# Gates and branches with the tokens stationary and 512 weight columns moving, the merged result turned on TensorE, and column sums and mixer steps placed anew

## The chip, the cores and the metric

One core of one Trainium2 chip runs the whole kernel. The metric is device time of one execution in microseconds (us), as the median of several executions. A profiled execution is slightly different from the timed ones; its own time stands beside its span below. Engines are called as the profile calls them: PE is TensorE (PEld its weight loads), DVE is VectorE, ACT is ScalarE, POOL is GpSimd, SP is SyncE, which issues the large loads.

## The reference, cut to what matters

256 tokens of width 2048 pass one encoder layer. All arithmetic is float32.

```
mod = silu(c) @ w_ada + b_ada                 # sh1, sc1, g1, sh2, sc2, g2, each 2048 wide
u = plain_norm(x) * (1 + sc1) + sh1
parts = split(u @ w_in)                       # inputs of the four mixers
y_a, y_b, y_c, y_d = pool(..), dsa(..), mla(..), conv(..)      # 512 wide each
gated = [sigmoid(u @ w_gate[i] + b_gate[i]) * (y @ w_branch[i])  for i, y in enumerate(...)]
merged = gated[0] + gated[1] + gated[2] + gated[3]
x = layer_norm(ALPHA * x + (1 + g1) * (merged @ w_o))
u2 = plain_norm(x) * (1 + sc2) + sh2
x = layer_norm(ALPHA * x + (1 + g2) * (silu(u2 @ wa) * (u2 @ wb)) @ w_ffn_out)
```

## The kernel before, in words

**Weights as a stream.** Weights come in loads of 1 MB (128 x 2048 float32) into three `raw` buffers (`RAW`). SP issues them in one fixed order (L1212). Each 128 x 1024 half of a load is one *unit*: ACT casts it to `wh` (L1242), DVE subtracts to get the rest `wl` (L1243), and PE multiplies high by high, high by low and low by high, so that each product of float32 matrices is three of fp32r. The preparation runs four units ahead of PE (`LEAD`), in five `wh` and five `wl` buffers. Every engine takes its instructions in the order in which this program writes them.

**Two ways to multiply.** `mm_B` (L393) keeps weights stationary and moves 256 tokens: 24 matmuls of 256 columns a unit, with features on the partitions of the result. `mm_A` (L418) keeps 128 tokens stationary and moves 512 weight columns: 12 matmuls of 512 columns a unit, with tokens on the partitions. `w_o` and the FFN go by `mm_A`; nearly all of `w_in`, the gates and the branches go by `mm_B`.

**The stages.** (1) The start: `w_ada` for sh1 and sc1 arrives in five segments among the first `w_in` units. DVE and POOL scale and sum its rows into `accd` and `accp`; PE turns the sum into columns (`adacol`, L263), DVE adds the bias (`modc`, L270 and L272), and `make_u` writes the high and low halves of u (`u0h`, `u0l`, ...), which all further units of those k need. (2) The rest of `w_in`, some 50 units, with the mixers beside it. The gate of branch 0 is computed here too (groups g of 10 and more). (3) Branch 0, then gate and branch of i = 3, 2 and 1: 48 loads of gates and 16 of branches, 128 units. (4) `w_o` and a norm. (5) The FFN.

**The ada rest.** 48 more loads of `w_ada` (the list `rest`) are strewn among the loads by `put_rest`, from load number `REST_FROM` of `w_in` on. For each load ACT scales two rows (L245, `gemv`) and POOL adds them to `accp` (L246).

**Side work.** The mixers are generators. After each unit, `run_side` advances each lane's first mixer; `yield n` means that its next step comes n units later (times the lane's pace), and `fins` holds the column sums, which run `FIN_DELAY` units after the sum is complete. A step puts its instructions on the engines' queues at that point of the program: a PE instruction of a step that is not ready holds all matmuls behind it. Column sums of squares (`rq`, `rkv`, `cvar`) are followed by a power on POOL (L151), a diagonal on DVE (L176) and a broadcast matmul on PE (`rbq`, `rbkv`, `cb`, L585).

**Slots.** Tiles of 128 x 1024 come from 30 slots; `drop` gives one back.

Of the kernel before, what the change touches and what calls it, by code (L numbers as in the profile page):

```python
# [74 lines left out]
def block_kernel(ctx: ExitStack, tc: tile.TileContext, a, out, dbg=None):  # L75
# [68 lines left out]
    bgh = cp.tile([P, 64], F32, name="bgh")  # L144
    dve.tensor_scalar(bgh, col("b_gate", 0, 64), 0.5, None, op0=OP.mult)
# [75 lines left out]
    def ada_items(srcs, width, on_dve, fin):  # L221
# [3 lines left out]
        def prep(i):  # L225
            def f(raw):
# [20 lines left out]
                if i == len(srcs) - 1:  # L247
# [6 lines left out]
                    fins.append([now[0] + FIN_DELAY, fin(ac), 1])  # L254
# [188 lines left out]
    def win_use(pi, g, k0, k1):  # L443
        def use(k, wh, wl):
# [6 lines left out]
            if g == 3:  # L451
# [37 lines left out]
    def gate_tanh(i, g, dst, src):  # L489
        for j in range(4):  # L490
            o = slice(j * 256, (j + 1) * 256)
            c = 16 * i + 4 * g + j
            act.activation(dst[:, o], src[:, o], AF.Tanh, scale=0.5, bias=bgh[:, c:c + 1])
# [4 lines left out]
    def seg_ada(si):  # L498
# [4 lines left out]
        return ada_items([a["ada1"][n0 + j] for j in range(n)], 512 if si < 2 else 1024, dv, seg_fin(si))  # L503
# [84 lines left out]
    def conv_mix():  # L588
# [34 lines left out]
        yield 2  # L623
# [44 lines left out]
    def rms(cq, nt, width, gname, name):  # L668
# [7 lines left out]
        yield 2  # L676
# [115 lines left out]
    def dsa_mix():  # L792
        iw, kp = idx["iw"], idx["kp"]
        yield 2
        sc_ = slot("score")
# [59 lines left out]
        drop(sc_, G.pop(1), G.pop(2), G.pop(3))  # L855
# [18 lines left out]
    def gate_use(i, g, kq):  # L874
        def use(half, wh, wl):
# [5 lines left out]
            mm_B(ps, wh, wl, act_u, ks, kq == 0 and half == 0, last)  # L881
            if last:
                T[i, g] = slot("T")
                gate_tanh(i, g, T[i, g], ps)
        return use

    def branch_use(i, g, first_i, last_i):
        def use(half, wh, wl):
# [500 lines left out]
```

## Time and profile before

| | us |
|---|---|
| median of 3 executions | 1735.74 |
| lowest and highest | 1734.02, 1741.04 |
| the profiled execution | 1733.01 |
| its span | 1731.2 |
| mean granted TensorE clock, share of full | 0.969 |

The span runs from the first to the last instruction. The page says how long each engine was busy, the windows say it for a stretch of time together with the granted clock and the DMA share, and the waits name who ended an engine's idle time. A matmul's duration overlaps the next, so the price of one is taken from start to start.

### The profile page before, as it was taken

To read this page: it belongs to the slowest core of one execution; us is meant where nothing else is said; L and a number is where in the kernel's file an instruction comes from. 1 tells how busy PE (TensorE), PEld (TensorE's weight loads), DVE (VectorE), ACT (ScalarE), POOL (GpSimd) and SP (SyncE) were. 2 spreads that over 40 slices of the span, in tenths; PEclk is the share of its full clock that TensorE was granted. 3 is DMA by queue.
4 is the path that set the end of the run, shared out by engine and by line. 5 is a ranking of instruction groups with operands and counts; after the bars stand their busy time and mean duration, and the time that the engine had idled before them with its cause. 6 is when DMAs were issued, how large, how long until landed. Compare 5 with 4: busy or idle time off the path is not lost.

```text
span 1731.2 us, 23941 instructions
## 1 busy us (share of the span) xinstructions
PE 1627.8 (94%) x9822; PEld 1462.7 (84%) x9822; DVE 1184.7 (68%) x1087; ACT 855.3 (49%) x1008; POOL 434.1 (25%) x194
## 2 busy tenths in 40 slices
PE   5789998977999999999999699999999999999996
PEld 5789998967999999989988588888888888888885
DVE  7698859895698698786766756676455555444556
ACT  5744545655666646656544454444443344444442
POOL 2422305664345575585302200000000000000001
PEclk8899989998999999999999799999999999999998
DMA  8877854464567667678666257777555555555661
GB/s 323 309 286 269 310 208 158 154 233 146 214 231 301 254 251 265 272 283 327 255 259 253 96 189 276 286 270 284 178 194 195 194 195 183 184 191 195 226 231 53
DMA packets 57854, 397.40 MB, mean 230 GB/s; under 512 B 6416, under 2 KB 6672, under 8 KB 11792
## 3 DMA queue, kind: packets, MB, share of 16 engines
q1 hardware_dynamic: 57456, 395.63, 62.3%
q8 instruction: 77, 1.26, 0.3%
q10 hardware_dynamic: 288, 0.23, 0.0%
q14 instruction: 33, 0.27, 0.0%
HBM read 393.74 MB, written 2.10 MB: 229 GB/s over the span
## 4 chain that ended last, share of the span: by engine, by line
PE 74%; DVE 10%; DMA 5%; issue 5%; ACT 3%; POOL 3%; ACTq 0%; DVEq 0%; POOLq 0%; SPq 0%
PE ffn L415 9%; PE ffn L416 9%; PE ffn L413 9%; PE tok L415 6%; PE tok L416 6%; PE tok L413 6%; PE gate L406 5%; PE gate L399 5%; PE gate L400 5%; DVE wl L1243 4%; DMA raw<-in_win_dram 4%; PE win L400 2%; PE win L399 2%; PE branch L399 2%; PE branch L406 2%
## 5 line engine op out<-in xcount | busy, mean ns | idle before, releaser
L1243 DVE TENSOR_TENSOR wl<-raw,wh 128x1024 fp32r<-128x1024 f32 x529 | 741.8, 1422 | 400.3 <-ACT wh L1242 399.4
L1242 ACT CAST wh<-raw 128x1024 fp32r<-128x1024 f32 x536 | 548.5, 1044 | 585.9 <-PE ffn L416 229.9
L246 POOL TENSOR_TENSOR accp<-accp,gemv 128x1024 f32<-128x1024 f32 (+1 forms) x118 | 322.8, 2736 | 321.7 <-ACT gemv L245 317.7
L151 POOL TENSOR_TENSOR rs_r<-rs_v,nhalf 128x1 f32<-128x1 f32 (+1 forms) x11 | 7.4, 676 | 785.5 <-DVE rs_v L149 785.5
L245 ACT ACTIVATE gemv<-raw,c_act 128x1024 f32<-128x1024 f32 (+1 forms) x118 | 128.3, 1122 | 55.8 <-DMA raw<-in_ada_dram 49.2
L240 DVE SCALAR_TENSOR_TENSOR accd<-raw,c_act,accd 128x1024 f32<-128x1024 f32 (+1 forms) x73 | 106.4, 1458 | 3.4 <-DMA raw<-in_ada_dram 2.1
L415 PE MATMUL ffn<-wl,v01h 128*128 128x512 f32 x176 | 69.8, 397 | 5.0 <-DVE wl L1243 5.0
L413 PE MATMUL ffn<-wh,v00h 128*128 128x512 f32 x176 | 71.4, 405 | 0.6 <-ACT v00h L1072 0.6
L416 PE MATMUL ffn<-wh,v00l 128*128 128x512 f32 x176 | 69.6, 396 | 1.5 <-DVE v00l L1074 1.5
L413 PE MATMUL ffn<-wh,v01h 128*128 128x512 f32 x176 | 70.2, 399 | 0.0
L413 PE MATMUL ffn<-wh,v10h 128*128 128x512 f32 x176 | 68.6, 390 | 1.4 <-ACT v10h L1072 1.4
L415 PE MATMUL ffn<-wl,v00h 128*128 128x512 f32 x176 | 69.5, 395 | 0.0
L416 PE MATMUL ffn<-wh,v01l 128*128 128x512 f32 x176 | 69.5, 395 | 0.0
L416 PE MATMUL ffn<-wh,v10l 128*128 128x512 f32 x176 | 68.6, 390 | 0.0
L415 PE MATMUL ffn<-wl,v10h 128*128 128x512 f32 x176 | 68.5, 389 | 0.0
L413 PE MATMUL ffn<-wh,v11h 128*128 128x512 f32 x176 | 68.5, 389 | 0.0
L415 PE MATMUL ffn<-wl,v11h 128*128 128x512 f32 x176 | 68.5, 389 | 0.0
L416 PE MATMUL ffn<-wh,v11l 128*128 128x512 f32 x176 | 68.5, 389 | 0.0
L399 PE MATMUL win<-u0h,wh 128*128 128x256 f32 x200 | 53.5, 301 | 13.8 <-ACT u0h L380 11.2
L610 POOL TENSOR_TENSOR cv<-cv,gemv 128x512 f32<-128x512 f32 x30 | 47.8, 1593 | 72.4 <-ACT gemv L608 71.6
L606 DVE SCALAR_TENSOR_TENSOR cv<-pad,wdw,cv 128x256 f32<-128x256 f32 x60 | 57.4, 996 | 0.0
L399 PE MATMUL win<-u1h,wh 128*128 128x256 f32 x200 | 50.8, 290 | 5.6 <-ACT u1h L380 5.6
(437 smaller groups left out, 4146.7 us busy)
## 6 DMA issues: line engine op xcount, KB each, us to landing
raw<-in_ada_dram SPq DMA_DIRECT2D x96, 1024.0 KB, 5.1
raw<-in_wfi_dram SPq DMA_DIRECT2D x88, 1024.0 KB, 4.8
raw<-in_win_dram SPq DMA_DIRECT2D x51, 1024.0 KB, 4.8
raw<-in_wgate_dram SPq DMA_DIRECT2D x48, 1024.0 KB, 5.0
raw<-in_wfo_dram SPq DMA_DIRECT2D x44, 1024.0 KB, 4.8
raw<-in_wbr_dram SPq DMA_DIRECT2D x16, 1024.0 KB, 4.9
raw<-in_wo_dram SPq DMA_DIRECT2D x16, 1024.0 KB, 5.5
x<-in_x_dram SPq DMA_DIRECT2D x4, 512.0 KB, 6.1
```

The lines of the kernel that those rows point to most:

```text
L240: dve.scalar_tensor_tensor(ac, w, cc, ac, op0=OP.mult, op1=OP.add)
L245: act.activation(tmp[:, :width], w, AF.Copy, scale=cc)
L246: pool.tensor_tensor(ac, ac, tmp[:, :width], op=OP.add)
L399: pe.matmul(o, w, xh, start=first and i == 0 and j % 2 == 0, stop=False, skip_group_check=True)
L400: pe.matmul(o, w, xl, start=False, stop=False, skip_group_check=True)
L406: pe.matmul(o, w, xh, start=False, stop=last and i == len(ks) - 1, skip_group_check=True)
L413: pe.matmul(o, h, rh, start=first and i == 0 and (width == 512 or t == 0), stop=False, skip_group_check=True)
L415: pe.matmul(o, h, rl, start=False, stop=False, skip_group_check=True)
L416: pe.matmul(o, l, rh, start=False, stop=last and i == len(ks) - 1, skip_group_check=True)
L606: dve.scalar_tensor_tensor(o, z, w, o, op0=OP.mult, op1=OP.add)
L1242: act.copy(wh[:, :n], raw)
L1243: (pool if half in it["on_pool"] else dve).tensor_tensor(wl[:, :n], raw, wh[:, :n].bitcast(F32), op=OP.subtract)
```

## The change

Gates and branches are multiplied by `mm_A` instead of `mm_B`. The results have tokens on the partitions, so the gate's bias is no longer a value for each partition: rows of `b_gate` are loaded, spread over all partitions (`load_bias`), and DVE adds them (`gate_bias`) before one tanh on ACT; before, ACT did bias and tanh in four pieces. The sum of the branches is turned on PE (`turn_m`) before it is split for `w_o`. Apart from that: column sums of the five segments run 4 instead of 7 units after their sum; the ada rest begins at load 52 instead of 38 of `w_in`; some yields are longer (2 to 4 units between the column sums and their broadcast, 3 to 4 ahead of the transposes of MLA), the pool mixer goes at half pace; and the scores of MLA and DSA lie in the two `pads` instead of slots.

```
-REST_FROM = 38
+REST_FROM = 52
 FIN_DELAY = 7
+SEG_DELAY = 4
 H_DELAY = 3
+M_DELAY = 3
...
-LANES = (((3, 1), (1, 2)), ((2, 1),), ((0, 1),))
+MLA_PACE = 1
+LANES = (((3, 1), (1, 2)), ((2, MLA_PACE),), ((0, 2),))
...
     def alloc_row(v, row):
         def f():
+            if v == 2:
+                finish(gens[1])
+                finish(gens[2])
...
-            if g == 3:
+            if g == 3 or g >= 10:
                 mm_A([ps[:, 0:512], ps[:, 512:1024]], wh, wl, act_u, ks, first, last)
...
-            if k0 == 0 and k1 < 16:
+            if k0 == 0 and g >= 10:
+                gate_bias(0, g - 10, dst, src)
+            elif k0 == 0:
                 act.copy(dst, src)
-            elif k0:
+            else:
                 dve.tensor_tensor(dst, src, dst, op=OP.add)
...
-                gate_tanh(0, g - 10, dst, dst if k0 else src)
+                act.activation(dst, dst, AF.Tanh, scale=0.5)
...
+    def load_bias(i, h):
+        def f():
+            brow[i, h] = slot(f"bg{i}{h}")
+            b = a["bgate"]
+            sync.dma_start(brow[i, h], bass.AP(tensor=b.tensor, offset=b.offset + i * D + h * 1024,
+                                               ap=[[0, P], [1, 1024]]))
+        return f
+
+    def gate_bias(i, g, dst, src):
+        b = brow[i, g // 2][:, (g % 2) * 512:(g % 2 + 1) * 512]
+        dve.tensor_tensor(q4(dst, 512), q4(src, 512), b[:, None, :].to_broadcast([P, 2, 512]), op=OP.add)
+        if g % 2 or (i, g) == (0, 2):
+            drop(brow.pop((i, g // 2)))
...
+        if i == 2:
+            C(load_bias(0, 0))
+            C(load_bias(0, 1))
+        if i == 106:
+            U(load_bias(0, 1))
...
         dg = row_bcast_diag(r, 0, "c")
-        yield 2
+        yield 4
...
-            Sx_ = slot("mS")
+            finish(gens[0])
+            Sx_ = pad_rows()[0]
...
             softmax(Sx, nk, "m")
-            yield 3
+            yield 4
...
-            mm_B(ps, wh, wl, act_u, ks, kq == 0 and half == 0, last)
+            mm_A([ps[:, 0:512], ps[:, 512:1024]], wh, wl, act_u, ks, kq == 0 and half == 0, last)
             if last:
-                T[i, g] = slot("T")
-                gate_tanh(i, g, T[i, g], ps)
+                t = T[i, g] = slot("T")
+                gate_bias(i, g, t, ps)
+                act.activation(t, t, AF.Tanh, scale=0.5)
...
+    def turn_m(g):
+        ps = mm_ps("mtp")
+        m = merged[g]
+        for j in range(4):
+            for t in range(2):
+                pe.transpose(ps[:, j * 256 + t * P:j * 256 + (t + 1) * P],
+                             m[:, t * 512 + j * P:t * 512 + (j + 1) * P], ident)
+        mh[g], ml[g] = split(ps, f"mg{g}", scale=0.5)
+        drop(m)
+        yield
...
-                mh[g], ml[g] = split(merged[g], f"mg{g}", scale=0.5)
-                drop(merged[g])
+                fins.append([now[0] + M_DELAY, turn_m(g), 1])
...
     def gate_items(i, g):
         for kq in range(4):
+            if g % 2 == 0 and kq == 2:
+                U(load_bias(i, g // 2))
```

Three places show what this does to the order of instructions.

On PE, where the last branch ends and `w_o` (`tok`) begins, the kernel before has this (`ybh` and `ybl` are the halves of the branch's input, `mg0h` and `mg0l` of the merged sum):

```order
L399 MATMUL branch<-ybh,wh 128x256
L400 MATMUL branch<-ybl,wh 128x256
L406 MATMUL branch<-ybh,wl 128x256 x8
L413 MATMUL tok<-wh,mg0h 128x512
L415 MATMUL tok<-wl,mg0h 128x512
L416 MATMUL tok<-wh,mg0l 128x512
```

and the changed kernel this (`mtp` is the turned sum):

```order
L417 MATMUL branch<-wh,ybh 128x512
L419 MATMUL branch<-wl,ybh 128x512
L420 MATMUL branch<-wh,ybl 128x512
L915 MATMUL mtp<-kcst,m_4042 128x128 x8
L417 MATMUL tok<-wh,mg0h 128x512
L419 MATMUL tok<-wl,mg0h 128x512
L420 MATMUL tok<-wh,mg0l 128x512
```

The branch now has the form of `w_o`, and eight transposes of a merged group stand between the two; one more group of eight follows two units later, and two stand among the gates and branches ahead.

On DVE, between the end of the sum of the second segment (L250, L251 now) and its bias (`modc`), the kernel before has this:

```order
L250 TENSOR_TENSOR accd<-accd,accp 128x512
L1243 TENSOR_TENSOR wl<-raw,wh 128x1024 x2
L238 TENSOR_SCALAR accd<-raw,c_act 128x1024
L1243 TENSOR_TENSOR wl<-raw,wh 128x1024 x2
L240 SCALAR_TENSOR_TENSOR accd<-raw,c_act,accd 128x1024
L1243 TENSOR_TENSOR wl<-raw,wh 128x544
L1243 TENSOR_TENSOR wl<-raw,wh 128x1024
L240 SCALAR_TENSOR_TENSOR accd<-raw,c_act,accd 128x1024 x2
L1243 TENSOR_TENSOR wl<-raw,wh 128x1024
L270 SCALAR_TENSOR_TENSOR modc<-adacol,cols 128x2
```

and the changed kernel this:

```order
L251 TENSOR_TENSOR accd<-accd,accp 128x512
L1279 TENSOR_TENSOR wl<-raw,wh 128x1024 x2
L239 TENSOR_SCALAR accd<-raw,c_act 128x1024
L1279 TENSOR_TENSOR wl<-raw,wh 128x1024
L507 TENSOR_TENSOR g_484<-win,bg_237 128x1024
L1279 TENSOR_TENSOR wl<-raw,wh 128x1024
L507 TENSOR_TENSOR g_505<-win,bg_237 128x1024
L271 SCALAR_TENSOR_TENSOR modc<-adacol,cols 128x2
```

The bias of the segment moved ahead of three parts of the next segment's sum and of three `wl`, and stands behind two of the new additions of the gate's bias.

On SP, in the second half of `w_in`, where the loads of the mixers' small weights (`wq`, `wp`, `wkv`) stand, the kernel before has this (`ada` is the ada rest):

```order
L1212 DMA raw<-in_ada_dram 128x2048
L537 DMA wp<-in_wpool_dram 128x512
L1212 DMA raw<-in_win_dram 128x2048 x2
L1212 DMA raw<-in_ada_dram 128x2048
L1212 DMA raw<-in_win_dram 128x2048
L1212 DMA raw<-in_ada_dram 128x2048
L1212 DMA raw<-in_win_dram 128x2048 x2
L1212 DMA raw<-in_ada_dram 128x2048
L537 DMA wkv_3201<-in_wkvup_dram 128x1024
```

and the changed kernel this, up to the first branch (`wbr`):

```order
L558 DMA wp<-in_wpool_dram 128x512
L1248 DMA raw<-in_win_dram 128x2048 x6
L558 DMA wkv_3108<-in_wkvup_dram 128x1024
L558 DMA wkv_3110<-in_wkvup_dram 128x1024
L1248 DMA raw<-in_win_dram 128x2048 x7
L1248 DMA raw<-in_ada_dram 128x2048
L1248 DMA raw<-in_win_dram 128x2048
L1248 DMA raw<-in_ada_dram 128x2048
L1248 DMA raw<-in_win_dram 128x2048
L1248 DMA raw<-in_ada_dram 128x2048
L501 DMA bg_3693<-in_bgate_dram 128x1024
L1248 DMA raw<-in_wbr_dram 128x2048 x2
```

Of the 48 loads of the ada rest, 11 stood among the loads of `w_in` and 37 among those of gates and branches; now it is 3 and 45. Nine loads of bias rows (`bg`, 0.5 MB each) are new, two of them near the start and seven from here on.

## Rows read from the trace of the kernel before

**Rows 1.** Page, part 1: engine, busy us, share of the span, instructions.
```profile
PE 1627.8 (94%) x9822; PEld 1462.7 (84%) x9822; DVE 1184.7 (68%) x1087; ACT 855.3 (49%) x1008; POOL 434.1 (25%) x194
```

**Rows 2.** Windows: stretch, length, busy us by engine, granted clock, DMA share, GB/s.
```profile
29.50:67.50 38.00, 37.98 (x286) 37.32 (x287) 27.22 (x26) 29.03 (x35) 14.03 (x8) 0.93 0.90 328
67.50:137.50 70.00, 51.41 (x362) 49.66 (x361) 59.11 (x47) 35.00 (x39) 24.73 (x9) 0.83 0.75 270
137.50:245.50 108.00, 106.12 (x825) 104.67 (x824) 85.84 (x68) 52.62 (x57) 28.52 (x12) 0.94 0.78 287
268.60:405.80 137.20, 119.75 (x822) 111.31 (x821) 120.58 (x120) 75.63 (x118) 85.56 (x49) 0.95 0.49 181
405.80:470.70 64.90, 53.09 (x390) 51.78 (x389) 37.58 (x37) 37.93 (x61) 23.85 (x11) 0.89 0.48 175
470.70:870.00 399.30, 395.84 (x3239) 391.09 (x3238) 314.01 (x264) 243.14 (x296) 221.88 (x80) 1.00 0.72 271
```

**Rows 3.** Waits of PE: line, releaser, us in total, times, longest.
```profile
PE win L399 <- ACT u0h L380: 11.2, 2, 9.5
PE rbkv L585 <- DVE diag L176: 8.1, 1, 8.1
PE cb L585 <- DVE diag L176: 6.2, 1, 6.2
PE win L399 <- ACT u1h L380: 5.6, 1, 5.6
PE ptr L657 <- DVE mS L647: 5.0, 1, 5.0
```

**Rows 4.** Timeline of PE in a gate: start us, us, the last eight matmuls of two successive units.
```profile
565.54 1.12 PE L406 MATMUL gate<-u2h,wl 128*128 128x256 f32 x8
...
568.42 1.12 PE L406 MATMUL gate<-u2h,wl 128*128 128x256 f32 x8
```

**Rows 5.** Timeline of PE in `w_o`: two matmuls twelve apart.
```profile
880.95 0.39 PE L413 MATMUL tok<-wh,mg2h 128*128 128x512 f32 x1
...
883.67 0.39 PE L413 MATMUL tok<-wh,mg2h 128*128 128x512 f32 x1
```

**Rows 6.** Timeline of DVE from 50 to 82 us.
```profile
51.66 0.69 DVE L250 TENSOR_TENSOR accd<-accd,accp 128x512 f32<-128x512 f32 x1 [1.20 <-POOL accp L246]
...
76.39 0.15 DVE L270 SCALAR_TENSOR_TENSOR modc<-adacol,cols 128x2 f32<-128x2 f32 x1
...
79.66 0.69 DVE L381 TENSOR_TENSOR u0l<-n,u0h 128x512 fp32r<-128x512 f32 x1 [1.32 <-ACT u0h L380]
```

**Rows 7.** Timelines of DVE and of POOL from 748 to 786 us.
```profile
759.57 6.65 DVE L1243 TENSOR_TENSOR wl<-raw,wh 128x1024 fp32r<-128x1024 f32 x2 [1.24 <-ACT wh L1242]
767.30 10.13 DVE L1243 TENSOR_TENSOR wl<-raw,wh 128x1024 fp32r<-128x1024 f32 x4 [1.07 <-ACT wh L1242]
...
761.75 13.46 POOL L246 TENSOR_TENSOR accp<-accp,gemv 128x1024 f32<-128x1024 f32 x4
```

**Rows 8.** By tile, 268.6 to 405.8 us: xcount, ns minimum/median/maximum, first and last start.
```profile
L606 DVE SCALAR_TENSOR_TENSOR cv<-pad,wdw,cv x56: 469/480/2648, 269.5 to 399.0; 128x256 f32<-128x256 f32 x56
L610 POOL TENSOR_TENSOR cv<-cv,gemv x28: 1262/1472/2282, 268.5 to 401.3; 128x512 f32<-128x512 f32 x28
...
L246 POOL TENSOR_TENSOR accp<-accp,gemv x13: 2347/2510/3388, 304.7 to 405.0; 128x1024 f32<-128x1024 f32 x13
```

**Rows 9.** By tile, 470.7 to 870 us, the same columns.
```profile
L1243 DVE TENSOR_TENSOR wl<-raw,wh x128: 1207/1225/3445, 469.7 to 863.6; 128x1024 fp32r<-128x1024 f32 x128
...
L246 POOL TENSOR_TENSOR accp<-accp,gemv x70: 2378/2792/3502, 474.3 to 843.8; 128x1024 f32<-128x1024 f32 x70
...
L906 POOL TENSOR_TENSOR m<-m,T x8: 2393/2408/3363, 607.7 to 759.4; 128x1024 f32<-128x1024 f32 x8
...
L813 DVE SCALAR_TENSOR_TENSOR score<-rtmp,iw,score x30: 340/484/2649, 473.2 to 523.1; 128x128 f32<-128x128 f32 x15, 128x256 f32<-128x256 f32 x15
```

**Rows 10.** Timeline of PE in the FFN: eight transposes of one group.
```profile
1034.62 1.03 PE L1099 MATMUL htp<-kcst,silu 128*128 128x128 f32 x8
```

More of the change, by code (lines that the diff above doesn't have):

```diff
@@ L37 @@
 _o = 0
-for _n, _w in (("c", 16), ("b_ada", 96), ("b_gate", 64), ("pool_scale", 4), ("q_norm", 3), ("kv_norm", 2),
+for _n, _w in (("c", 16), ("b_ada", 96), ("pool_scale", 4), ("q_norm", 3), ("kv_norm", 2),
                ("b_dw", 4), ("conv_ln_g", 4), ("conv_ln_b", 4), ("w_dw", 124)):
@@ L143, in block_kernel @@
     dve.tensor_scalar(wdw, col("w_dw", 0, 124), 0.5, None, op0=OP.mult)
-    bgh = cp.tile([P, 64], F32, name="bgh")
-    dve.tensor_scalar(bgh, col("b_gate", 0, 64), 0.5, None, op0=OP.mult)
     def rstd_of(var, n, scale=1.0):
@@ L218, in finish, with ada_items @@
             lst[:] = [e for e in lst if e[1] is not g]
-    def ada_items(srcs, width, on_dve, fin):
+    def ada_items(srcs, width, on_dve, fin, delay=FIN_DELAY):
         cell = {}
@@ L253, in f @@
                         ac, = cell.values()
-                    fins.append([now[0] + FIN_DELAY, fin(ac), 1])
+                    fins.append([now[0] + delay, fin(ac), 1])
             return f
@@ L487, in block_kernel @@
     T = {}
[L489 to L493, printed above, removed]
+    brow = {}
+    def load_bias(i, h):
[10 more added lines that the diff above has]
+            drop(brow.pop((i, g // 2)))
     def U(fn):
@@ L502, in seg_ada @@
         dv = lambda k: k % m == 0
-        return ada_items([a["ada1"][n0 + j] for j in range(n)], 512 if si < 2 else 1024, dv, seg_fin(si))
+        return ada_items([a["ada1"][n0 + j] for j in range(n)], 512 if si < 2 else 1024, dv, seg_fin(si), SEG_DELAY)
     first = seg_ada(0)
@@ L675, in rms @@
         drop(sq)
-        yield 2
+        yield 4
         b = bcast_ps(dg, "rb" + name)
@@ L780, in mla_mix @@
             softmax(Sx, nk, "m")
-            yield 3
+            yield 4
             yield from pv(Sx, nk, vt, y, qt, "m")
-            drop(Sx_)
             yield 2
@@ L794, in dsa_mix @@
         yield 2
-        sc_ = slot("score")
+        finish(gens[3])
+        sc_ = pad_rows()[1]
         for qt in range(2):
@@ L854, in dsa_mix @@
             yield 2
-        drop(sc_, G.pop(1), G.pop(2), G.pop(3))
+        drop(G.pop(1), G.pop(2), G.pop(3))
         Y[1] = split(y, "yb")
@@ L894, in use @@
             yh, yl = Y[i]
-            mm_B(ps, wh, wl, tokB([yh], [yl]), [2 * half, 2 * half + 1], half == 0, half == 1)
+            mm_A([ps[:, 0:512], ps[:, 512:1024]], wh, wl, tokB([yh], [yl]), [2 * half, 2 * half + 1], half == 0,
+                 half == 1)
             if half == 0:
@@ L1278 @@
         ("ada1", (32, P, 2048)), ("ada2", (4, 2, 8, P, 2048)),
-        ("win", (len(WUNITS) // 2, P, 2048)),
+        ("bgate", (4, D)), ("win", (len(WUNITS) // 2, P, 2048)),
         ("wpool", (P, 512)), ("wqup", (P, 2304)), ("wkvup", (P, 2048)),
@@ L1321, in colm @@
         return v.reshape(-1, P).T
-    cols = [colm(g["c"][0]), colm(g["b_ada"][0]), colm(g["b_gate"][0].reshape(-1)), colm(g["pool_scale"][0]),
+    cols = [colm(g["c"][0]), colm(g["b_ada"][0]), colm(g["pool_scale"][0]),
             colm(g["q_norm"][0]), colm(g["kv_norm"][0]), colm(g["b_dw"][0]), colm(g["conv_ln_g"][0]),
@@ L1360, in _layout @@
         x=g["x"][0], cols=np.concatenate(cols, 1), kc=_consts(), rows=rows, ada1=ada1, ada2=ada2,
-        win=win,
+        win=win, bgate=g["b_gate"][0],
         wpool=g["w_pool"][0].transpose(1, 0, 2).reshape(P, 512),
```

## The prediction

> **What bounds the kernel now.** I began with the page's first part: PE is busy 94% of the span, no other engine over 68% [rows 1]. PE's instruction stream is the thing to shorten, but 94% is a mean over stages, so the windows by stage came next [rows 2]. They show three kinds of stretch. From 470.7 to 870 us (gates and branches) PE is busy 395.84 of 399.30 us at the full clock: what PE saves there is saved, if nothing else is as full. From 29.5 to 67.5 us DMA is at a share of 0.90 and 328 GB/s; after that it falls to 270 and 287 GB/s while PE is idle for 18.6 of 70 us, so DMA bounds the start and is itself held up by PE's waits, because buffers fill. From 268.6 to 470.7 us (the mixers beside the second half of `w_in`) PE idles 17.4 and 11.8 us, the granted clock is 0.95 and 0.89 (so some 10% and 22% of the time at 1.2 instead of 2.4 GHz), and DMA is at half its share. The waits of PE name the causes: u0h and u1h in the start, the diagonals and the softmax of MLA in the mixers [rows 3]. Third, I asked what is nearly full beside PE. Rows 7 answer: six `wl` on DVE and four `accp` on POOL, both reading two tiles of SBUF, stretch each other. Four `accp` take 13.46 us there, 3.36 each, and DVE makes one `wl` in the same time, though either alone takes 1.21 and 2.38 us at its least [rows 9]. They take turns, so an `accp` costs the pair 3.36 - 1.21 = 2.15 us of a shared resource, which I call the port.
>
> The Trainium skill, page "SBUF — State Buffer", section "Who interferes with whom", says that a DVE instruction with two SBUF inputs and a GpSimd instruction that reads SBUF exclude each other for whole instructions. By that rule, the trace agrees.
>
> **1. The 512 form.** Two successive gate units stand 568.42 - 565.54 = 2.88 us apart, 120 ns for each of 24 matmuls [rows 4]; twelve matmuls of `w_o`, with the same 6144 columns, take 883.67 - 880.95 = 2.72 us [rows 5]. That is 0.16 us a unit. The change gives it to 128 units of gates and branches (20.5 us), to 20 gate units of branch 0 beside the mixers (3.2 us) and to 12 in the start, where DMA bounds and I count nothing.
>
> [...]
>
> **2. Gates and branches, 399.3 us.** PE's floor: 395.84 - 20.5 = 375.3; the MLA steps that slip in from ahead (estimated at 3.5 us, the length of some twenty small matmuls and a column sum) and two turns. A turn is eight transposes; they start at 1034.62 and take 1.03 us with the overlap at the end [rows 10], so I take 0.9 us each. Floor: 380.6 us. The port's floor: 128 `wl` at 1.21 make 155; POOL adds 70 `accp` and 8 merged products now [rows 9], and 8 more loads of the ada rest bring 16 multiplications, of which one opens a sum on ACT, so 85 + 8 adds at 2.15 make 200; 30 index scores at some 0.42 make 13, and other two-input work about 10 (an estimate from the few remaining instructions of that kind). Together 378 us; before it was 155 + 168 + 28 = 351, of 399. So PE at 380.6 and the port at 378 become bounds together, where PE alone was one. Two queues that meet so closely wait for each other more than one at 88% did; I add 10 us and take 390 us: a gain of 9, between 18.7 (no added wait) and a loss of 12 (the 401 of rival A and the 10). The new addition of the gate's bias (16, some 1.2 us each, as a `wl` of the same size) reads PSUM and so isn't on the port; it takes DVE time that `wl` leaves (314 us of 399 busy), and ACT gives back a little. It makes DVE wait for the last matmul of a gate; behind it stands the `wl` of a unit four units ahead, 10.9 us of cover, so I count nothing; without cover a wait of a few tenths, 16 times. The seven loads of bias rows make 118 MB in 390 us, 303 GB/s, under the 328 of the start.
>
> **3. Mixers, first part, 137.2 us.** PE's floor is 119.75 us less half of the 13.7 us at the half clock and less 1.3 us for eight gate units: some 112 us. The port carries 13 `accp` there, and they are gone in the changed order: 13 x 2.15 = 28 us. What else it carries (56 conv sums on DVE at 0.47, 28 on POOL at 1.26 [rows 8], some 30 `wl` at 1.21) makes 98, and with the 28 nearly fills the stretch, so the removal counts: 137.2 - 28 = 109. The waits for the diagonal (8.1 us for `rbkv`) get two more units, 5.8 us, and POOL's queue is shorter. I take 114 us, a gain of 23, between 10 (the delays don't meet and the conv chain sets the pace) and 25.
>
> **4. Mixers, second part, 64.9 us.** The waits for `cb` (6.2 us) and `ptr` (5.0 us) get 5.8 and 2.9 us more, and clock falls go with long idle times: busy 53.1 us less some 7 at the half clock is 46. Twelve gate units give 1.9 us, and 3.5 us of MLA move on. I take 51 us, a gain of 14, between 5 and 20.
>
> **5. The start.** The sum of the second segment is complete at 52.4 us; its bias comes at 76.39, and u0l begins at 79.66 [rows 6], while PE waits 9.5 us [rows 3]. The bias stood on DVE behind `wl` and parts of the next segment that waited for DMA. Four units instead of seven, and fewer of those ahead, bring u0h before PE asks for it; the 5.6 us for u1h go the same way. What is late next is DMA: the 18.9 MB of the stretch from 67.5 to 137.5 take 57.6 us at 328 GB/s, a gain of 12.4, from which the two new bias loads (1.05 MB) take 3.2. After that PE is busy 106 of 108 us. I take 10, between 0 (the column sums now wait on PE for the same loads) and 16.
>
> **6. After that.** Two turns ahead of and in `w_o` cost 1.8 us; the split after them reads PSUM at the price it had. The last one is two units after its sum and 6.8 us ahead of its use. 2 us lost, between 1 and 5.
>
> **The sum.** -9 - 23 - 14 - 10 + 2 = -54 us. The profiled execution took 1733.0 us, 2.7 below the median, so 1679 there and 1682 as a median. All best ends together gain 18.7 + 25 + 20 + 16 - 1 = 79 us, which gives 1657; all worst, 10 + 5 + 0 - 12 - 5 = -2, give 1738.
>
> **Rivals.** (A) The port bounds the gates. In a stretch without mixers two units need 1.5 adds: 1.5 x 3.36 + 0.5 x 1.21 = 5.65 us, where PE needs 5.44. 64 loads make 361.6, merged products 17, the rest 23: 401, so nothing is gained there, 11 us more than I take: 1693. For it: while POOL is full, a `wl` comes every 3.36 us [rows 7], later than PE asks for it. Against it: with the mixers' matmuls a load has 380.6 / 64 = 5.95 us on PE, more than 5.65. (B) PE is the only bound: gates 380.6, start and mixers at their best ends: 1682 - 9 - 6 - 8 = 1659. For it: PE stood still for only 3.5 us at a port load of 88%. (C) Slower: SP is a queue in order, and six of the bias loads among the gates wait for PE or POOL to let go of a slot; behind each stand the raw loads. Three buffers cover two loads. From 54 / 6 = 9 us of PE's time for each on, this decides; the last readers are at most four units off, 10.9 us, which would give 1682 + 65 = 1747. Against it: slots go around in order, so their readers are mostly long done. (D) The change doesn't do what it says: the fixed 13 ns of a matmul doesn't fall with their number in a gate, whose stationary operand now alternates between tokens; gates 403, mixers 3 more: 1698. Against it: `w_o` does the same already. (E) The delays move the stalls: the diagonals wait elsewhere, 25 of the 37 us of parts 3 and 4 stay: 1707.
>
> **Chances.** My forecast, 1670 to 1690: 0.52; A 0.18; B 0.15; C 0.05; D 0.03; E 0.07. About 0.5%, 8.7 us, is what a measurement can tell from no change. All but C, and E where A and no gain in the start come with it (0.04), are faster by more: 0.91 faster, 0.04 within, 0.05 slower. The range from 1657 to 1710 leaves out C and E's end with A; B's time is inside.
>
> **What would show it.** Right: gate units 2.72 us apart; no wait for u0h near 80 us; the conv stretch at about 114 us, POOL without `accp` in it; the clock at full from there on; in the gates more `wl` over 3 us and new waits of PE for `wl`, some 10 us. Wrong: gate units at 2.88 us (D); PE at the column sums instead of u0h; the gates at 400 us with POOL full (A); SP's bias loads issued late with PE idle behind them (C).

## The result: slower by 1.1%

The changed kernel takes 1755.72 us (median of 4 runs, 1753.46 to 1759.32) against 1737.49 us for the kernel before beside it (4 runs, 1734.02 to 1741.04): a ratio of 1.0107, with an interval of 1.0078 to 1.0136. The forecast was 1682, in a range from 1657 to 1710. The profiled execution has a span of 1754.9 us, 23.7 more than before.

The page's first part, for the changed kernel:

```profile
PE 1620.1 (92%) x7934; PEld 1355.8 (77%) x7934; DVE 1206.7 (69%) x1102; ACT 844.4 (48%) x957; POOL 445.8 (25%) x194
```

PE has fewer instructions and is busy for 8 us less in all [rows 1], and yet the span is longer: PE waits more, and part of its busy time is at the lower clock. The windows by stage say where (stretch, length, busy us by engine, granted clock, DMA share, GB/s). The borders are the first matmul that reads u3 (237.0 us), the first branch of i = 0 (430.7) and the first of `w_o` (894.8):

```profile
29.50:67.50 38.00, 33.76 (x205) 30.82 (x206) 28.34 (x28) 26.61 (x34) 13.38 (x8) 0.90 0.89 331
67.50:137.50 70.00, 61.17 (x428) 57.45 (x427) 63.46 (x49) 35.84 (x39) 25.17 (x9) 0.93 0.79 286
137.50:237.00 99.50, 94.34 (x675) 89.71 (x675) 78.99 (x65) 49.68 (x54) 29.13 (x12) 0.97 0.81 293
237.00:430.70 193.70, 182.26 (x1132) 163.62 (x1132) 147.84 (x166) 105.13 (x162) 69.54 (x46) 0.97 0.48 170
430.70:894.80 464.10, 410.45 (x1774) 321.82 (x1772) 365.71 (x286) 256.71 (x283) 277.66 (x95) 0.96 0.70 258
```

The same window of the mixers in the kernel before, whose borders are 239.2 and 470.7 us (its gates stand in [rows 2]):

```profile
239.20:470.70 231.50, 200.70 (x1419) 190.67 (x1420) 177.01 (x175) 127.50 (x199) 113.09 (x61) 0.93 0.47 172
```

So the start ends 2.2 us earlier, the mixers take 193.7 us instead of 231.5 (37.8 less), and the gates and branches 464.1 instead of 399.3 (64.8 more). The rest is about a microsecond shorter. In the gates PE is busy for 410 of 464 us at a granted clock of 0.96, a mean of its two levels: some 8% of the stretch at 1.2 GHz, where it had 1.00 before.

The waits of PE (line, releaser, us in total, times, longest):

```profile
PE gate L419 <- DVE wl L1279: 25.8, 40, 2.6
...
PE mtp L915 <- DVE m L941: 7.6, 1, 7.6
PE dl L865 <- DVE modc L271: 7.4, 1, 7.4
PE qn L731 <- DVE g L701: 6.5, 1, 6.5
```

The waits of before for u0h, the diagonals and the softmax [rows 3] are gone or short. The largest in these stages is now one that was not in that list: gates that wait for `wl`, forty times. `mtp` and `dl` wait for DVE as well.

Two `wl` matmuls twelve apart in a branch show that the 512 form itself does what it should where nothing is late: 885.79 - 883.07 = 2.72 us, against 2.88 for a unit in [rows 4].

```profile
883.07 0.39 PE L419 MATMUL branch<-wl,ybh 128*128 128x512 f32 x1
...
885.79 0.39 PE L419 MATMUL branch<-wl,ybh 128*128 128x512 f32 x1
```

Why is `wl` late? Three readings. The first is a group view of DVE and POOL in the gates (line, operation, tiles, shapes, count | busy us, mean ns | idle before), and the same view of `wl` before the change:

```profile
L1279 DVE TENSOR_TENSOR wl<-raw,wh 128x1024 fp32r<-128x1024 f32 x130 | 277.8, 2172 | 85.3 <-ACT wh L1278 85.3
...
L247 POOL TENSOR_TENSOR accp<-accp,gemv 128x1024 f32<-128x1024 f32 x85 | 254.0, 2989 | 149.0 <-ACT gemv L246 145.2
```

```profile
L1243 DVE TENSOR_TENSOR wl<-raw,wh 128x1024 fp32r<-128x1024 f32 x128 | 235.9, 1882 | 75.2 <-ACT wh L1242 75.0
```

A `wl` takes 2172 ns as a mean, where it took 1882 before, and its lower bound in [rows 9] is 1207. While POOL adds without a pause, PE gets its `wl` at the pace of such a pair (timeline of PE):

```profile
781.29 0.50 PE L419 MATMUL gate<-wl,u0h 128*128 128x512 f32 x1 [0.32 <-DVE wl L1279]
784.64 0.50 PE L419 MATMUL gate<-wl,u0h 128*128 128x512 f32 x1 [0.32 <-DVE wl L1279]
788.00 0.50 PE L419 MATMUL gate<-wl,u1h 128*128 128x512 f32 x1 [0.34 <-DVE wl L1279]
```

These waits stand 3.35 us apart, where a unit needs 2.72. In the gates and branches 28 successive pairs of them stand 3.32 to 3.37 us apart; before the change there were two such pairs. It is the 3.36 us that a `wl` and an `accp` took together in [rows 7].

DVE also sits idle for 85 us until ACT has cast `wh`, 10 us more than before. So the third reading is ACT's waits in the same window:

```profile
ACT gemv L246 <- DMA raw<-in_ada_dram: 50.1, 17, 6.2
ACT T L907 <- DVE T L507: 48.5, 12, 5.4
ACT wh L1278 <- DMA raw<-in_wgate_dram: 35.6, 29, 5.3
```

Twelve times the tanh of a gate waits for DVE's addition of the bias (L507), 4 us each. This wait didn't exist before. The timelines around one of them (start us, us, engine, line, operation, count, idle before and its releaser; POOL, DVE, ACT, PE):

```profile
773.52 13.34 POOL L247 TENSOR_TENSOR accp<-accp,gemv 128x1024 f32<-128x1024 f32 x4
...
779.51 9.57 DVE L1279 TENSOR_TENSOR wl<-raw,wh 128x1024 fp32r<-128x1024 f32 x4 [1.63 <-ACT wh L1278]
789.00 1.21 DVE L507 TENSOR_TENSOR T<-gate,bg 128x1024 f32<-128x1024 f32 x1
794.35 8.30 DVE L1279 TENSOR_TENSOR wl<-raw,wh 128x1024 fp32r<-128x1024 f32 x3 [4.14 <-ACT wh L1278]
...
790.24 1.06 ACT L907 ACTIVATE T<-T 128x1024 f32<-128x1024 f32 x1 [5.43 <-DVE T L507]
791.21 2.17 ACT L246 ACTIVATE gemv<-raw,c_act 128x1024 f32<-128x1024 f32 x2
793.29 1.98 ACT L1278 CAST wh<-raw 128x1024 fp32r<-128x1024 f32 x2
...
787.04 0.39 PE L420 MATMUL gate<-wh,u0l 128*128 128x512 f32 x1
...
793.12 0.39 PE L420 MATMUL gate<-wh,u1l 128*128 128x512 f32 x1
794.37 0.50 PE L417 MATMUL gate<-wh,u2h 128*128 128x512 f32 x1 [0.86 <-ACT wh L1278]
```

The gate's last matmul starts at 787.04 us, so its sum is complete at some 787.4. The bias addition stands on DVE's queue behind four `wl`, stretched by POOL's `accp` to 9.57 us, and starts at 789.00. ACT has come to the tanh long before and sits idle for 5.43 us; behind the tanh stand two multiplications for the ada rest, and only then, at 793.29, the next `wh`. DVE then waits 4.14 us for that `wh`, and PE waits for it at 794.37. DVE had cover here; ACT had none.

### The profile page after: what moved, and what is told of

Read it like the earlier page. It is cut to its first block, busy times and chain, and to the rows that moved or that the text cites. A ratio compares the mean times of both kernels' runs of the same rounds, so it can differ in the third digit from the quotient of the medians.

```text
span 1754.9 us, 20111 instructions
## 1 busy us (share of the span) xinstructions
PE 1620.1 (92%) x7934; PEld 1355.8 (77%) x7934; DVE 1206.7 (69%) x1102; ACT 844.4 (48%) x957; POOL 445.8 (25%) x194
## 4 chain that ended last, share of the span: by engine, by line
PE 62%; DVE 16%; DMA 9%; issue 6%; ACT 5%; POOL 2%; SPq 0%; ACTq 0%; DVEq 0%; POOLq 0%
PE ffn L419 9%; PE ffn L420 9%; PE ffn L417 9%; DVE wl L1279 9%; PE tok L420 6%; PE tok L419 6%; PE tok L417 6%; DMA raw<-in_wgate_dram 4%; DMA raw<-in_win_dram 3%; ACT wh L1278 2%; PE win L403 2%; PE win L404 2%; PE win L410 2%; DVE accd L241 2%; ACT gemv L246 2%
## 5 line engine op out<-in xcount | busy, mean ns | idle before, releaser
L1279 DVE TENSOR_TENSOR wl<-raw,wh 128x1024 fp32r<-128x1024 f32 x529 | 774.6, 1482 | 414.2 <-ACT wh L1278 412.4
L247 POOL TENSOR_TENSOR accp<-accp,gemv 128x1024 f32<-128x1024 f32 (+1 forms) x118 | 334.6, 2837 | 307.8 <-ACT gemv L246 303.6
L419 PE MATMUL gate<-wl,u2h 128*128 128x512 f32 x96 | 40.3, 420 | 11.0 <-DVE wl L1279 11.0
L477 DVE TENSOR_TENSOR g<-win,g 128x1024 f32<-128x1024 f32 (+1 forms) x36 | 42.3, 1174 | 5.8 <-PE win L410 4.0
L419 PE MATMUL gate<-wl,u3h 128*128 128x512 f32 x96 | 39.7, 414 | 6.5 <-DVE wl L1279 6.4
```

What stands on the lines that cost most here:

```text
L247: pool.tensor_tensor(ac, ac, tmp[:, :width], op=OP.add)
L419: pe.matmul(o, h, rl, start=False, stop=False, skip_group_check=True)
L1279: (pool if half in it["on_pool"] else dve).tensor_tensor(wl[:, :n], raw, wh[:, :n].bitcast(F32), op=OP.subtract)
```

## Experiments

Theory H (hold-up): what is seen in that timeline. Theory P (port): 15 more additions on POOL [rows 9], 85 instead of 70, and DVE's `wl` shut each other out. Theory W (early `wl`): the 512 form asks for `wl` earlier within a unit. The table gives all runs; the stages are read from the profiled executions by the same first matmuls as above. That is one execution for each kernel, and executions of one kernel lie up to 21 us apart (e1: 1725.69 to 1746.84); e4, e7, e8, e12 and e13 were timed only twice. So differences of a few us between stages are not clear of chance, and sums below that agree to 1 us do so in part by luck.

| kernel | median us | ratio to before (interval) | mixers us | gates and branches us |
|---|---|---|---|---|
| before | 1737.49 | | 231.5 | 399.3 |
| after | 1755.72 | 1.0107 (1.0078 to 1.0136) | 193.7 | 464.1 |
| e1 late tanh | 1731.49 | 1.0019 (0.9978 to 1.0059) | 196.1 | 434.4 |
| e2 no bias, i = 1 to 3 | 1736.95 | 1.0031 (0.9993 to 1.0069) | 194.7 | 437.8 |
| e3 ada rest from 38 | 1744.86 | 1.0100 (1.0024 to 1.0176) | 218.4 | 429.0 |
| e4 `wl` last | 1761.51 | 1.0170 (1.0107 to 1.0232) | 195.9 | 464.8 |
| e5 placement alone | 1725.39 | 0.9940 (0.9902 to 0.9978) | 197.5 | 433.8 |
| e6 late tanh, rest from 38 | 1724.94 | 0.9958 (0.9928 to 0.9988) | 216.4 | 400.1 |
| e7 ada sums on DVE | 1703.65 | 0.9839 (0.9798 to 0.9879) | 195.6 | 405.6 |
| e8 late tanh, ada sums on DVE | 1692.58 | 0.9775 (0.9746 to 0.9803) | 192.6 | 399.6 |
| e9 placement alone, ada sums on DVE | 1698.69 | 0.9796 (0.9754 to 0.9839) | 199.0 | 402.4 |
| e10 as e8, rest from 38 | 1693.48 | 0.9774 (0.9725 to 0.9822) | 207.0 | 384.4 |
| e11 before, ada sums on DVE | 1703.60 | 0.9830 (0.9785 to 0.9875) | 211.9 | 393.5 |
| e12 as e1, without POOL's ada sums | 1684.90 | 0.9710 (0.9659 to 0.9761) | 193.8 | 386.9 |
| e13 as e8, ada rows not read | 1672.42 | 0.9638 (0.9597 to 0.9679) | 192.1 | 381.7 |

The kernel before took from 1731 to 1737 us in these comparisons; ratios are each to its own.

**e1: the tanh three units later.** The tanh goes to `fins`, so that ACT's next casts stand ahead of it.

```diff
-                act.activation(t, t, AF.Tanh, scale=0.5)
+                late_tanh(t)
...
+    def late_tanh(t):
+        def g():
+            act.activation(t, t, AF.Tanh, scale=0.5)
+            yield
+        fins.append([now[0] + TANH_DELAY, g(), 1])       # TANH_DELAY = 3
```

> The changed kernel; the tanh of each gate is issued three units after the addition of its bias instead of right behind it. The stretch from the first branch to w_o is 464 us in the changed kernel and 399 in the kernel before. Theory H (hold-up): the tanh waits on ACT for DVE's bias addition, which stands behind the wl of four units ahead (ACT stood still 48.5 us in 12 such waits), and ACT's next casts and scalings stand behind the tanh: the wait goes, and the stretch falls by 30 to 50 us, the time to 1705 to 1725. Theory P (port): the 16 more additions of the ada rest on POOL share the port with wl: nothing changes, 460 us, 1750 to 1757. Theory W (early wl): the 512 form asks for wl with its second matmul instead of its seventeenth: nothing changes either.

```profile
438.70:873.10 434.40, 401.86 (x1773) 322.31 (x1772) 354.08 (x286) 258.19 (x283) 275.67 (x95) 0.97 0.74 276
```

Gates and branches fall by 29.7 us, just short of the 30 to 50 that H expected. The whole gains less, 21.2 us in the profiled execution and 24.2 in the medians, and misses the time expected: in this execution the start ends at 242.6 us instead of 237.0 and the mixers take 2.4 us more. H is real, and it isn't the whole.

**e2: the gates of i = 1 to 3 without their bias.** ACT takes the tanh from PSUM, as before; the rows of bias are still loaded.

```diff
-                gate_bias(i, g, t, ps)
-                act.activation(t, t, AF.Tanh, scale=0.5)
+                act.activation(t, ps, AF.Tanh, scale=0.5)
```

> The changed kernel without the gate's bias in branches 1 to 3 (left out of the result): ACT takes the tanh straight from PSUM, the bias rows are still loaded. Theory H: as with the late tanh or better, since DVE's 12 additions go as well: stretch 410 to 430 us. Theory P and theory W: 12 additions of 1.2 us on DVE that don't touch the port go; 450 to 462 us.

26.3 us less in the gates, between the two ranges expected and nearly e1's. With the additions gone the stage is no better than with the additions made and the tanh late: the wait that they caused on ACT costs, not DVE's own time for them (1.21 us each, as the timeline has it).

**e3: the ada rest from load 38 on, as before the change.**

```diff
-REST_FROM = 52
+REST_FROM = 38
```

> The changed kernel with the ada rest from load 38 on again: 11 instead of 3 of its 48 loads in the mixers, 37 instead of 45 among gates and branches. Theory P: 15 additions fewer at 2.15 us and more on DVE: the stretch of gates falls by 32 us or more, to 430 or less; the mixers give back some 25 us. Theory H: 5 to 15 us in the gates, 25 lost in the mixers, so slower than the changed kernel, 1760 to 1775.

The gates fall by 35.1 us and the mixers rise by 24.7. Fifteen `accp` fewer among the gates at the port price of part 2, 2.15 us each, would be 32 us: P's price of an addition about holds, and all of it comes out as time. The loads and ACT's products went with the additions here; e12 parts them.

**e4: `wl` last in a unit.** All eight matmuls with `wh` go first, then the four with `wl`.

> The changed kernel with the same matmuls in gates and branches, in another order: the eight with wh first, then the four with wl, so wl is asked for 1.8 us into a unit instead of 0.23 us. Theory W: PE's waits for wl (25.8 us in 40) go, and so do the slow units: stretch 425 to 440 us. Theory H and theory P: what PE doesn't wait for wl it waits for wh: 455 to 464 us.

464.8 us: W falls. What PE no longer waits for `wl` it waits for `wh`, 20.1 us in 12 waits of the gates. The tanh still waits as it did (line, releaser, us in total, times, longest):

```profile
ACT T L920 <- DVE T L520: 51.9, 12, 7.5
```

**e5: the placement alone.** The kernel before, with the delays, lanes, `REST_FROM` and slots of the change, but 256 columns moving, the bias in the tanh and no turns.

```diff
-REST_FROM = 38
+REST_FROM = 52
...
+SEG_DELAY = 4
...
-LANES = (((3, 1), (1, 2)), ((2, 1),), ((0, 1),))
+LANES = (((3, 1), (1, 2)), ((2, 1),), ((0, 2),))
...
-        yield 2
+        yield 4
...
```

> The kernel before with the placement alone: ada rest from load 52, four units' delay of the segments' column sums, the longer yields, the pool mixer's pace, scores in the pads; gates and branches stay with weights stationary. The late tanh and the earlier ada rest each gave back about 30 us of the 65 that gates and branches lost. Theory P (port): 16 more additions on POOL slow this stretch here too, from 399 to 425 or more; the mixers gain 38, total 1715 to 1725. Theory H (hold-up through the tanh, which here waits for PE alone): 399 to 410 us, total 1695 to 1705.

```profile
436.50:870.30 433.80, 409.16 (x3286) 401.04 (x3285) 346.69 (x270) 262.83 (x322) 269.37 (x95) 0.98 0.73 268
```

The placement alone makes nearly all of both shifts: 34.0 us gained in the mixers, 34.5 lost in the gates, where there is neither a bias addition nor a 512 form. 399.3 + 34.5 + 29.7 (H, from e1) is 463.5, and the changed kernel took 464.1. So the 512 form, with the bias additions and turns that it needs, gave nothing in the gates: e1, which has it and no hold-up, takes 434.4 us and e5 433.8.

**e6 and e7, e8: the cures together.** e6 is e1 with e3's edit. e7 puts the sums of the ada rest on DVE, where one instruction multiplies and adds, so that both POOL's additions and ACT's multiplications go; e8 is e7 with the late tanh.

```diff
-            rest += ada_items([...], 1024, lambda k: False, f(v, h))
+            rest += ada_items([...], 1024, lambda k: True, f(v, h))
```

> The changed kernel with the late tanh and with the ada rest from load 38. If hold-up and port are two causes that add up: gates and branches 464 - 30 - 35 = 399 us, mixers 219, total 1712 to 1720. If they are one cause told twice: 425 us, total 1740.

> The changed kernel; the ada rest is scaled and added on DVE (one instruction of some 1.28 us for each row) instead of on ACT and POOL, with as many loads at the same places. Theory P: the 85 additions leave the port to wl (no wl over 1.3 us but by chance), stretch 425 to 435 us, the hold-up of the tanh stays. If the additional loads cost as DMA or as raw buffers and not by the port: 455 to 465 us. DVE's own load is against it: 85 x 1.28 = 109 us more.

> The changed kernel with both: late tanh and ada rest on DVE. Two causes that add up: gates and branches 390 to 400 us, total 1690 to 1705, faster than both kernels. If DVE is then the bound, with 128 wl at 1.21, 85 sums at 1.28 and 75 us of the rest making 340 us in the order of the program: 410 to 425 us, total 1710 to 1725.

```profile
454.50:854.60 400.10, 388.59 (x1758) 317.36 (x1756) 332.90 (x282) 239.97 (x263) 223.50 (x80) 0.99 0.75 277
```

```profile
430.60:830.20 399.60, 388.08 (x1773) 319.39 (x1773) 350.76 (x373) 161.80 (x193) 25.89 (x10) 0.99 0.81 299
```

e6: 464.1 - 29.7 - 35.1 = 399.3 by the sum of e1 and e3, 400.1 measured: two costs that add up; the median of the kernel, 1724.94, is above the 1712 to 1720 expected. e7 takes 58.5 us off the gates, more than e3, and ends at 405.6 us, under both ranges expected; besides POOL's additions it removes ACT's products (93.5 us of ACT's time), so it doesn't tell which of the two did it. In e8 the two edits don't add up (464.1 - 29.7 - 58.5 would be 376): the stage stays at 399.6. e8 beats both kernels: 0.9775, some 40 us less than the one before.

**e9, e10, e11: what is the bound then?** e9 is e5 with e7's edit, e10 is e8 with `REST_FROM = 38`, e11 the kernel before with e7's edit.

> The placement alone with 256 columns moving (as in e5), and the additions of the ada rest on DVE instead of POOL. Theory P+PE: with the additions off the port, TensorE is the bound of gates and branches again, and there the form of the matmul counts. 3072 matmuls at the 120 ns of [rows 4] make 368.6 us; the steps beside them took 31.6 us in e8, and 20 us of waits and slow matmuls were left: gates and branches 420 us where e5 took 433.8, and the kernel about 1718. Rival Q: the queues set the pace whatever the form, so the stage takes the 400 us of e8, and the kernel about 1698.

> e8 with the ada rest begun as early as before the change (37 of its loads among the gates instead of 45). Theory PE: e8's gates and branches are bounded by TensorE, so eight loads fewer there take away only their sixteen column-sum matmuls and part of a wait, 3 to 5 us: 395 to 397. Rival Q: DVE's queue or the DMA buffers set the pace; eight of 108 megabytes and of DVE's additions fewer make 375 to 385. The mixers lose by it what e3 and e6 lost, 22 to 24 us, if the loads themselves cost that, and under 10 if POOL's additions did, which are not made here. Time: 1705 to 1712 by PE and loads, 1675 to 1690 by Q and POOL.

> The kernel before with one edit: the additions of the ada rest on DVE instead of POOL. Theory P+PE: gates and branches can lose only their waits, so they stay between 390 and 399 us; in the mixers the 13 additions on POOL go, which the prediction priced at 28 us in all: 205 to 215 us instead of 231.5, and the kernel 1705 to 1722. Rival: what costs there is the loads and their multiplications, not POOL's additions, so the mixers stay at 225 to 232 and the kernel at 1722 to 1732.

```profile
434.50:836.90 402.40, 399.10 (x3287) 395.77 (x3286) 336.04 (x359) 167.76 (x227) 25.67 (x10) 1.00 0.77 288
```

```profile
243.60:450.60 207.00, 187.76 (x1148) 167.68 (x1149) 171.72 (x191) 100.27 (x163) 59.05 (x41) 0.95 0.57 201
450.60:835.00 384.40, 381.76 (x1758) 317.22 (x1756) 330.97 (x356) 162.49 (x187) 25.88 (x10) 1.00 0.78 287
```

```profile
237.50:449.40 211.90, 195.85 (x1419) 186.34 (x1420) 175.90 (x198) 105.29 (x179) 58.80 (x41) 0.95 0.53 194
449.40:842.90 393.50, 393.50 (x3239) 390.52 (x3238) 311.65 (x336) 166.51 (x220) 24.25 (x10) 1.00 0.74 273
```

The 402.4 us of e9 are the number of rival Q, but by the other mechanism: PE is busy for 399.10 us of them, at the full clock. It is the bound, as P+PE had it; the 20 us of waits that I had added from e8 were not there. e8 and e9 have the same placement and the same sums on DVE and differ by the form, its bias and turns and the late tanh: 2.8 us of the stage. e10 falls with PE's theory for e8: eight loads fewer take 15.2 us, not 3 to 5. So e8's 400 us are not PE's but a queue's (Q), while in e10 PE is busy for 381.76 of 384.40 us. Its mixers lose 14.4 us, between the two values expected, so neither the loads nor POOL's additions alone account for that. e10's time, 1693.48 us, is e8's: what one stage wins the other loses. e11 came out as P+PE says, in both stages; its 1703.6 us are a hair below the range given. Taking POOL's sums away is worth 5.8 us in the gates of the kernel before and 19.6 in its mixers.

**e12 and e13: additions, multiplications, or bytes?** e12 is e1 with ACT's products made and POOL's additions left out. e13 is e8 with DVE's instructions on the ada rows left out, but for the first of each sum, and all rows loaded.

```diff
-                        pool.tensor_tensor(ac, ac, tmp[:, :width], op=OP.add)
+                        if on_dve(k) is not None:
+                            pool.tensor_tensor(ac, ac, tmp[:, :width], op=OP.add)
...
-            rest += ada_items([...], 1024, lambda k: False, f(v, h))
+            rest += ada_items([...], 1024, lambda k: None, f(v, h))
```

```diff
-                        else:
+                        elif on_dve(k) != 2:
                             dve.scalar_tensor_tensor(ac, w, cc, ac, op0=OP.mult, op1=OP.add)
...
-            rest += ada_items([...], 1024, lambda k: False, f(v, h))
+            rest += ada_items([...], 1024, lambda k: 2, f(v, h))
```

> e1 (late tanh) with POOL's additions of the ada rest left out: 90 of its loads' halves are still loaded and multiplied on ACT, only the sums on POOL aren't made (so the modulation of the FFN is not the reference's). Theory P: the additions on POOL, which share SBUF's port with DVE's wl, are what cost the 35 us that e3 and e6 won back by fewer loads and the 35 that e8 won by moving them to DVE; gates and branches then fall from 434.4 us to the 400 of e8 or under, and the kernel to about 1697. Rival M: it is ACT's multiplications, which e8 also took away (DVE multiplies and adds in one instruction) and which stand on ACT's queue among the wh casts; they are still there, so gates and branches stay at 425 to 434, the kernel at 1722 to 1732.

> e8 (late tanh, additions on DVE) with all of the ada rest's products and sums but the first of each left out: its raw tiles are loaded and not read (so the modulation of the FFN is not the reference's). DVE loses some 100 us of work in the gates, DMA moves the same bytes. Theory S1: e8's 400 us in gates and branches, 20 of them waits and slow matmuls of TensorE, come from DVE, which is busy 351 of 400 us; then the stage falls to TensorE's own 380 to 386, and the kernel to 1671 to 1677. Theory S2: they come from DMA, 119 MB at 299 GB/s; then the stage stays at 395 to 400 and the kernel at 1686 to 1691.

```profile
433.00:819.90 386.90, 382.69 (x1772) 317.60 (x1771) 236.87 (x284) 258.95 (x283) 21.31 (x10) 1.00 0.84 309
```

```profile
428.80:810.50 381.70, 381.70 (x1772) 317.89 (x1772) 241.55 (x288) 164.87 (x187) 23.80 (x10) 1.00 0.83 311
```

e12: 386.9 us, 47.5 under e1, with ACT as busy as there (259 us). So rival M falls, and P stands: POOL's additions were the cost. Nor did they cost it by keeping ACT's product buffers: ACT waits for POOL only 4.4 us in e1 (5.5 in the changed kernel). The group views of e1, e12 and e8 show what the additions did to `wl`, 2072 ns as a mean with them and 1269 and 1254 without:

```profile
L1286 DVE TENSOR_TENSOR wl<-raw,wh 128x1024 fp32r<-128x1024 f32 x130 | 265.0, 2072 | 67.2 <-ACT wh L1285 67.2
```

```profile
L1287 DVE TENSOR_TENSOR wl<-raw,wh 128x1024 fp32r<-128x1024 f32 x128 | 159.0, 1269 | 128.6 <-ACT wh L1286 128.5
```

```profile
L1286 DVE TENSOR_TENSOR wl<-raw,wh 128x1024 fp32r<-128x1024 f32 x128 | 156.6, 1254 | 29.4 <-ACT wh L1285 29.1
L242 DVE SCALAR_TENSOR_TENSOR accd<-raw,c_act,accd 128x1024 f32<-128x1024 f32 x85 | 119.6, 1408 | 3.8 <-DMA raw<-in_ada_dram 2.2
```

e13: 381.7 us, with 311 GB/s of the same bytes: S1 holds and S2 falls. What held e8 at 400 was DVE's work: 120 us of ada sums on its queue ahead of or between the `wl`, or the raw buffers kept until DVE comes to them, and not the transfer of the bytes; which of these two it is, e13 doesn't tell apart. In e13 PE is busy for all of the 381.70 us. PE's waits for `dl` and `mtp`, 7.4 and 7.6 us in the changed kernel, are 0.8 and 1.9 in e12 and none in e13: they came from DVE's queue as well.

## Why the prediction was wrong

**1. The 512 form: right on PE, but not worth its 20.5 us.** Units 2.72 us apart were predicted and are there where nothing is late, and rival D is refuted with them. e13 has PE at 381.7 us without a wait, and the placement with 256 columns has PE busy for 399.1 (e9). These two floors lie 17.4 us apart, where 20.5 less 1.8 for the turns were predicted. But only where PE bounds the stage is that time won. In the changed kernel it was not, and e5's 433.8 us and the hold-up's 29.7 make 463.5 without the new form.

**2. Gates and branches: the step that failed.** PE's floor of 380.6 us was right to 1.1 us (e13). What the queues add to it was put at "10 us", and it is 82: 464.1 - 381.7. The runs split it: 29.7 us for the hold-up of ACT (after to e1), 47.5 us for POOL's additions (e1 to e12), 5.2 for what is left of the rest (e12 to e13, hardly more than chance). Two sentences of that part are wrong.

- "behind it stands the `wl` of a unit four units ahead, 10.9 us of cover, so I count nothing". It looked at the queue behind the waiting instruction on DVE, and not at the second engine that waits for it. DVE's addition stands *behind* the four `wl` made ahead, and the tanh on ACT waits for it, with the next `wh` behind the tanh. Cover on one queue was none on the other. So the four units of lead, which were to cover the wait, are what the addition stands behind; no run varied the lead.
- "PE at 380.6 and the port at 378 become bounds together". The sum had the right instructions (85 `accp`, 8 merged products, some 128 `wl`) at a price that e3 bears out, and took their total as the time in which the stage could be done. Without the hold-up the stage took 434.4 us (e1; 433.8 in e5): 378 of 434 is 87%. For before the change the prediction has 351 of 399, 88%; there it takes 28 us for the other work where its 378 takes 23, and like for like it is 346, again 87%. PE bounded the stage then, so that number alone doesn't show a limit; e6 does. It has the 70 additions of before and a PE that needs 381.7 us, and the stage still takes 400.1. So what I read as room ("more than one at 88% did") was as full as this chain gets. The kernel before stood at the edge of both bounds: with POOL's sums gone PE alone takes 393.5 us there (e11), 5.8 less. In hindsight, the same total divided by 0.88 gives 430 us, and with the hold-up 460. That the lost eighth goes into the ring of raw buffers (`wl` waits for `wh`, `wh` for a load, a load for a buffer that an earlier `wl` lets go) fits the waits of DVE and ACT above, but no run varied the buffers.

The Trainium skill, page "SBUF — State Buffer", section "Who interferes with whom", has DVE instructions with two SBUF inputs and GpSimd instructions that read SBUF exclude each other. The mean `wl` of 2072 ns with POOL's sums (e1) and of 1269 ns without them (e12) agrees.

**3 and 4. The mixers: right.** 23 and 14 us were predicted, 37 together, and 37.8 measured. The sums of the conv mixer on POOL part this (count, ns minimum/median/maximum, first and last start; before, then after):

```profile
L610 POOL TENSOR_TENSOR cv<-cv,gemv x30: 1262/1481/2282, 263.3 to 401.3; 128x512 f32<-128x512 f32 x30
```

```profile
L631 POOL TENSOR_TENSOR cv<-cv,gemv x30: 1265/1442/2280, 256.8 to 376.4; 128x512 f32<-128x512 f32 x30
```

From first to last they take 119.6 us instead of 138.0, a gain of 18.4 where part 3 took 23; after them 15.1 us are gained, where part 4 took 14, and 4.3 ahead of them, which the prediction did not forecast. So the total is closer than its parts. The waits for the diagonals and the softmax went; two others came in their place, `qn` at 6.5 us and `kn` beside it, as rival E has it for a small part. 24.7 of the 37.8 us come from the ada rest (e3). That is near the 28 us of part 3, which priced POOL's additions alone; but those are worth 19.6 us in the kernel before (e11), and loads whose sums are on DVE still cost 14.4 (e10), so the port is not all of it. And the work was not removed, it was moved into the stage where it costs more.

**5. The start: the mechanism right, the size not.** u0h no longer holds PE for 9.5 us (1.7 instead, as DVE's u0l begins at 69.0 us and not at 79.66). Yet the start ended only 2.2 us earlier, where 10 were taken: from 67.5 to 137.5 us DMA moves 286 GB/s, not the 328 on which the 12.4 us rested. PE's idle time from 29.5 us to the end of the start is 18.2 us instead of 19.0: instead of u0h and u1h its `win` matmuls now wait for ACT and DVE to take the sums `g` (13.1 us in seven waits) and for `wh` (4.0 us). So the waits moved, as rival E has it for the mixers. What holds `g` back wasn't tried; in the runs above the start ends between 235.5 and 243.6 us, so 2 us may be chance.

**6. The turns: nothing at `w_o`, a wait in the gates.** `w_o` begins 99.0 us ahead of the FFN as against 99.3 before. But the first turn makes PE wait 7.6 us (`mtp`) for DVE's last addition to its merged group, which stands among the `wl` on DVE; that counts in the gates, and the 0.9 us for a turn had no wait in it.

**Rivals.** A had the right mechanism for one of the two costs: PE waits for `wl` at the 3.36 us of a pair, 28 times in the changed kernel and 9 times still in e1. What spoke against it, 5.95 us of PE for a load, is a mean over the stage, and the additions come in bursts. Its 401 us missed what the queues lose between them. B's PE floor is what e13 shows, when DVE and POOL are emptied. C, the only one slower than the kernel before, did not occur: SP waits for a slot of a bias row once, for 0.3 us. No rival asked who else waits for DVE's addition.

## What to carry to other kernels

An instruction that waits for the end of a unit must be asked for on every queue in its chain: what stands ahead of it (all the work that was prepared in advance), and which engine's next preparation stands behind its *result*. A shared resource that the sum puts at 87% of the stage was full in this chain of engines with three load buffers; price work that is moved into such a stage by what the stage loses, not by the room left in a sum. And before a shorter instruction form is credited, take away the other bound: here POOL's sums moved to DVE were worth 28 us in the kernel before, by themselves, and the form, the other delays and the late tanh only some 10 us more on top of that (e10 against e11).

## What was not expected of the hardware

- DVE multiplies and adds a 128 x 1024 row with two SBUF inputs in 1.41 us as a mean (e8), where ACT's product and POOL's sum took some 1.1 and 2.99 us, and DVE's `wl` beside them 0.8 us more each (e1 against e12). The idle second engine was dearer than the busy one.
- The clock falls with PE's longer waits in the gates. Of the changed kernel's matmuls those at 571.7 and 574.3 us come after waits of 2.5 us for `wh` and 2.1 for `wl`, and that at 623.9 us after 2.6 us for `wl`. The granted clock is 0.50, the lower level of 1.2 GHz, in the stretches that begin there (stretch, length, busy us by engine, clock, DMA share, GB/s):

```profile
572.60:579.40 6.80, 5.15 (x14) 4.10 (x14) 6.80 (x3) 4.04 (x4) 6.09 (x3) 0.50 0.45 153
623.80:627.20 3.40, 3.33 (x8) 2.66 (x9) 3.25 (x8) 1.53 (x3) 3.32 (x2) 0.50 0.29 123
```

The other falls in this stage stand at the waits for `ptr`, `dl` and `mtp` (4.3, 7.4 and 7.6 us); together some 34 us are at the lower level, so at most 17 of the 82 us above are matmuls at the lower clock. The mean is 1.00 in the gates of e9, e10, e12 and e13, where at most one wait of that length is left (3.3 us in e9, 2.6 in e10).
